# Hybrid decoder trunk on one core: order of the first loads, the step-size projection in fp32 column quarters, and half of the samples' work moved to mid-group in the SSD scan

## The chip, the core and the metric

One NeuronCore of one Trainium2 chip. The metric is the device time of one execution of the whole program in microseconds (us). The kernel before takes 1557.68 us, the median of three runs (1556.93, 1557.68 and 1560.6). One further execution was taken with the hardware profiler.

## The reference

Two layers over 512 prompt tokens and 8 samples of 8 tokens each, all in fp32, model width 1024. Layer 0 has a Conformer convolution beside sliding-window attention; layer 1 has a Mamba-2 mixer. After either comes a gated feed-forward part with a width-3 convolution. The Mamba mixer, where most of the change lies, computes:

```python
z, xbc, dt = jnp.split(h @ w_in, [D_INNER, D_INNER + SSM_CONV_DIM], axis=-1)
xbc = jax.nn.silu(causal_dwconv(concat(conv_hist, xbc), conv_w, conv_b))
xs, bm, cm = jnp.split(xbc, [D_INNER, D_INNER + gn], axis=-1)
dt = jax.nn.softplus(dt + dt_bias)              # 32 heads
y, new_ssm = ssd_scan(xs, dt, -jnp.exp(a_log), bm, cm, ssm_hist)
y = (y + d_skip[:, None] * xs) * jax.nn.silu(z) # then grouped RMSNorm, @ w_out
```

`ssd_scan` cuts the 512 prompt tokens into four chunks of 128. With `acum` the running sum of `dt * a`, it weighs `C B^T` with `exp(acum_l - acum_s)` inside a chunk (the decays), carries a state of 128 x 64 per head from chunk to chunk, and returns the last state. Each sample starts from a state of its own and returns a new one.

## The kernel before

**Layout.** Activations lie with channels on the partitions and the 576 tokens (512 prompt, then 64 sample tokens) along the free axis, in two halves of 288. Every projection is done in three TensorE passes on split operands (`mm3`, lines 166 to 174): a weight tile is rounded to a high part `wh` on ScalarE (L162) and the rest `wl` is made on VectorE (L163); activations are split likewise into `hh` and `hl` (L182, L183). One unit is 128 output channels: 8 blocks x 3 passes x 2 halves = 48 matmuls of 288 columns. Raw weights come through three buffers `wr` (L152), all by the SP queue.

**Order.** The instructions are written out in Python; a compile-time scheduler then gives each engine a fixed order, in which it may take later instructions earlier where it expects their inputs to be ready. DMAs are issued by the SP queue in its own fixed order: an issue that waits for its buffer holds up all behind it.

**Slots.** Working tiles come from a list of slots of one size: 48, and from the first feed-forward part on 11 more (`EXTRA`). `S()` (L65) takes the slot that was freed longest ago; `free()` puts one back at the end of the list. A tile therefore waits for the last reader of whatever lay in its slot before.

**Start.** `setup` (from L108) sends the first weight columns (L152, 256 of them), then the eight x tiles (L126). `mix0` scales and splits each x tile on ScalarE and VectorE (L371, L372).

**Layer 1, `mix1` (from L837).** The norm of h is applied half by half (`norm_half`, L241): `hf = x * gain * rs` (L247), split to `hh`, `hl`. The first three units are then run together: the step sizes dt (256 weight columns, 32 outputs, in 48 matmuls of `mm3` like the others), B and C of group 0; first half 0 of all three, then half 1 (`units`, L257). dt is copied out as `dtr` (L874), transposed to tokens by TensorE (L895, L896), and goes through softplus and running sums to `acd` in DRAM, from which decays are read back broadcast over partitions.

**The scan, `ssd(g)` (L977), four groups of eight heads.** The head of a group: tokens of B (L984); the sample parts (L988 to L1022): copies of B and x for the samples three times over (`r3`), transposed and split into `b3` and `x3`, for both halves of the samples; C B^T masked (`cbm`, L1030); tokens of x times dt (`xdt`, L1037 to L1048, the fifth for the samples); chunk states (L1051 to L1074, the last one stored by L1072); the sample decays `es` (L1076 to L1083). Then four turns t, two heads each: `decays` loads a broadcast row `acb` (L1090), subtracts and exponentiates it on ScalarE (L1094, L1095) and masks it on VectorE (L1096); `outputs` multiplies it with `xdt` into `yp` (L1126); `carried` (L1107 to L1115) prepares the part from the state. `load` (L1141) fetches four sample states, `begin` (L1148, four column quarters of the array) multiplies them with C, `turn` and `finish` (L1165, L1178 to L1182) update and store them: the first four samples after t = 1, the other four after t = 3. Last, `ysp` (L1213) adds the samples' own tokens. `run` (L1253) interleaves this generator, at its yields, with other units (z, or the out-projection of the group before), which fill TensorE.

Of the kernel before, what the change touches and what calls it, by code (L numbers as in the profile page):

```python
# [9 lines left out]
F32R = mybir.dt.float32r  # L10
AF = mybir.ActivationFunctionType
# [3 lines left out]
P = 128  # L15
NP = 512
T = 576
# [23 lines left out]
for _name, _w in (  # L41
    ("ident", 128), ("rsc", 6), ("l1", 128), ("l2", 128), ("h32", 32), ("m32", 32), ("prot", 128), ("blk2", 2), ("blk8", 36), ("amask", 256), ("smask", 2 * 192),
    ("tri", 128), ("tris", 64), ("bmat", 64), ("bsel", 8), ("selx", 256), ("selm", 128),
    ("sel3", 192), ("bsel3", 4),
):
    CV[_name] = _n
    _n += _w
# [3 lines left out]
class Builder:  # L51
    NSLOT = 48
    EXTRA = 11
# [58 lines left out]
    def setup(self):  # L112
        nc, d = self.nc, self.d
        self.par = self.const.tile([P, NPV], F32, name="par")
        self.ident = self.const.tile([P, P], F32, name="ident")
        self.rsc = self.const.tile([P, 6], F32, name="rsc")
        self.l1 = self.const.tile([P, P], F32R, name="l1")
        nc.sync.dma_start(self.par[:, 0:8], d["par"][:, 0:8])
        self.x = []
        for k in range(8):  # L120
            t = self.xp.tile([P, T], F32, tag=f"x{k}", bufs=1, name=f"x{k}")
            self.x.append(t)
        self.pre = []
        self.pre.append(self.weights_load(d["w_in_e"][4][:, 0:256], 256))
        for k in range(8):
            nc.sync.dma_start(self.x[k], d["x"][k])  # L126
            if k == 1:
                nc.sync.dma_start(self.pre[0][:, 256:], d["w_in_e"][4][:, 256:])
            if k == 4:
                self.pre.append(self.weights_load(d["w_in_e"][0], 1024))  # L130
        self.pre.append(self.weights_load(d["w_in_e"][5], 1024))
        nc.sync.dma_start(self.ident, d["cst"][:, 0:128])
        nc.sync.dma_start(self.rsc, d["cst"][:, CV["rsc"]:CV["rsc"] + 6])
        l1 = self.S("l1f")
        nc.sync.dma_start(l1[:, 0:P], d["cst"][:, CV["l1"]:CV["l1"] + P])
# [12 lines left out]
        nc.scalar.activation(warm, self.eps, AF.Sqrt)  # L148
# [75 lines left out]
    def norm_begin(self, gname, early):  # L224
        self.gname, self.early = gname, early
        self.ssq, self.rs = self.S("ssq"), self.S("rs")
        self.h = [self.pair("h") for _ in range(8)]

# [11 lines left out]
    def norm_half(self, half):  # L240
        nc = self.nc  # L241
        sl = HALF[half]
        self.rstd(self.rs, self.ssq, self.o1024, sl)
        if not self.early:
            for k in range(8):
                t = self.S("hf")
                nc.vector.scalar_tensor_tensor(t[:, sl], self.x[k][:, sl], self.pv(self.gname, k), self.rs[:, sl],  # L247
                                               op0=MUL, op1=MUL)
                self.split(t[:, sl], self.h[k], sl)
                self.free(t)  # L250
        if half == 1:
            self.free(self.ssq)
# [4 lines left out]
    def units(self, todo, lead, ready=()):  # L257

        for u0 in (0,) + tuple(range(lead, len(todo))):
            grp = todo[:lead] if u0 == 0 else todo[u0:u0 + 1]  # L260
            ws = ready if ready and u0 == 0 else [self.weights(src, 8 * m) for src, m, _ in grp]
# [575 lines left out]
    def mix1(self):  # L837
# [33 lines left out]
        dtr = self.S("dtr", T, rows=32)  # L871

        def dt_evac(half, p):
            nc.scalar.activation(dtr[:, HALF[half]], p[0:32, :HB], AF.Copy)  # L874
# [19 lines left out]
        for c in range(4):  # L894
            nc.tensor.transpose(pt[:, c * 32:(c + 1) * 32], dtr[:, c * P:(c + 1) * P], self.ident[0:32, 0:32])  # L895
        nc.tensor.transpose(pt[0:64, 128:160], dtr[:, NP:], self.ident[0:32, 0:32])  # L896
# [22 lines left out]
        ea = self.Z("ea", 32, bufs=1)  # L919
# [4 lines left out]
        da = self.Z("da", W, bufs=1)  # L924
        nc.vector.scalar_tensor_tensor(da.rearrange("p (c h) -> p c h", h=32), dt.rearrange("p (c h) -> p c h", h=32), -1.0,
                                       ea.unsqueeze(1).broadcast_to([P, 5, 32]), op0=MUL, op1=MUL)
        dab = self.Z("dab", 256, rows=64, bufs=1)
# [20 lines left out]
        eas = self.Z("eas", 32, rows=64, bufs=1)  # L948
# [7 lines left out]
        dtde, dd3 = self.Z("dtde", 32, rows=64, bufs=1), self.Z("dd3", 64, rows=96, bufs=1)  # L956
# [4 lines left out]
        nc.vector.tensor_copy(dd3, pe[0:96, 0:64])  # L961

# [14 lines left out]
        def ssd(g):  # L977
# [8 lines left out]
            nc.scalar.activation(btok, pt, AF.Copy)  # L986

            r3 = []  # L988
            for a in [bf] + xs:
                r3.append(self.S("r3", 192))  # L990
                nc.scalar.activation(r3[-1].rearrange("p (b r t) -> p b r t", r=3, t=32),
                                     a[:, NP:T].rearrange("p (b t) -> p b t", t=32).unsqueeze(2).broadcast_to([P, 2, 3, 32]),
                                     AF.Copy)
            rep3 = lambda i, bh: r3[i][:, bh * 96:bh * 96 + 96]
            pt = self.ps("pt")
            b3 = []
            for bh in range(2):
                o = pt[0:96, bh * P:(bh + 1) * P]
                nc.tensor.transpose(o, rep3(0, bh), self.ident)
# [3 lines left out]
                b3.append(self.S("b3", NP, F32R, rows=96))  # L1003
# [4 lines left out]
            x3 = []  # L1008
            for bh in range(2):
                pt = self.ps("pt")  # L1010
                for t in range(4):
                    nc.tensor.transpose(pt[0:96, t * P:(t + 1) * P], rep3(1 + t, bh), self.ident)
# [3 lines left out]
                x3.append(self.S("x3", NP, F32R, rows=96))  # L1016
# [3 lines left out]
                yield  # L1020
            self.free(r3)
# [11 lines left out]
            self.free(bf)  # L1033
# [3 lines left out]
            for c in range(5):  # L1037
# [8 lines left out]
                xdt.append(o)  # L1046
                if c % 2:
                    yield  # L1048
# [3 lines left out]
            for c0 in (0, 2):  # L1052
# [9 lines left out]
                for c in (c0, c0 + 1):  # L1062
# [3 lines left out]
                    else:  # L1066
# [9 lines left out]
            es = self.S("es", NP, rows=64)  # L1076
            nc.sync.dma_start(es.rearrange("p (h l) -> p h l", l=64),
                              acd[8 * g:8 * g + 8, NP:T].partition_broadcast(64))
            l64 = lambda ap: ap.rearrange("p (h l) -> p h l", l=64)
            nc.vector.tensor_tensor(l64(es), l64(es), ac[0:64, hs(4)].unsqueeze(2).broadcast_to([64, 8, 64]), op=SUB)  # L1080
            nc.vector.tensor_scalar(es, es, 0.0, None, op0=MIN)
            nc.scalar.activation(es, es, AF.Exp)
            nc.vector.tensor_tensor(l64(es), l64(es), cbm[0:64, NP:].unsqueeze(1).broadcast_to([64, 8, 64]), op=MUL)  # L1083
# [88 lines left out]
            def finish(bh, behind):  # L1172

                for b0 in (0, 2):
# [4 lines left out]
                    self.tc.keep_in_program_order(m)  # L1179
                    for b4 in (b0, b0 + 1):  # L1180
                        nc.vector.tensor_tensor(h0[bh][b4], h0[bh][b4], pst[b4 - b0], op=ADD)
                        nc.sync.dma_start(d["ssm_s"][4 * bh + b4, g], h0[bh][b4])  # L1182
                        self.free(h0[bh][b4])
                    yield

            for t in range(4):
                if t == 0:
                    load(0)
                if t == 0:
                    ea2 = carried(0, False)  # L1190
                pair = []
# [15 lines left out]
                else:  # L1207
                    begin(t // 2)
            ysp = self.ps("ysp", "ysp")
# [9 lines left out]
            self.free(x3, b3)  # L1219
# [110 lines left out]
def constants():  # L1330
# [41 lines left out]
    put("tris", (same & (tt[:, None] <= tt[None, :])).astype(f))  # L1372
    put("bmat", same.astype(f))
# [110 lines left out]
```

## Time and profile before

| what | value |
|---|---|
| median of three runs | 1557.68 us |
| the profiled execution | 1559.9 us |
| its span, first to last instruction | 1558.1 us |
| TensorE (PE) busy | 1525.8 us, 98% |
| VectorE (DVE) busy | 1018.8 us, 65% |
| ScalarE (ACT) busy | 648.9 us, 42% |
| mean granted TensorE clock | 0.995 |
| moved by DMA | 157.78 MB, 101 GB/s |

[...] Busy times of PE are of overlapping matmuls: a busy PE can still run slower than it might, so the start-to-start distance of matmuls is read beside them. A wait is put down to the engine whose signal came last.

### The profile page before, as it was taken

How to read it: one execution, taken by the hardware profiler on the slowest of the kernel's cores; microseconds unless marked ns; L12 is line 12 of the kernel's file. 1: busy time of each engine (PE TensorE's matmuls, PEld its weight loads, DVE VectorE, ACT ScalarE, POOL GpSimd, SP SyncE). 2: the span in 40 equal slices, each digit the busy share in tenths (PEclk: the TensorE clock that was granted, in tenths of full speed). 3: DMA queues.
4: the chain of work that ended last, by engine and by line, in shares of the span. 5: the costliest groups of instructions: out<-in, count | busy, mean ns of one | idle time of the engine just before them, and what ended most of it. 6: DMA issues, size and time to landing. Idle time of an engine off the chain costs nothing.

```text
span 1558.1 us, 28566 instructions
## 1 busy us (share of the span) xinstructions
PE 1525.8 (98%) x11646; PEld 1454.2 (93%) x11646; DVE 1018.8 (65%) x1806; ACT 648.9 (42%) x1233; POOL 154.4 (10%) x365
## 2 busy tenths in 40 slices
PE   7999999999999999999999999999999999999999
PEld 7967799999999999898988988998899999999999
DVE  7968887653555464677896786777976644663552
ACT  6356563221222222576854754656542222221220
POOL 0036001000000000101211102102010000000000
PEclk9999999999999999999999999999999999999999
DMA  8515222222222222136245245235222222223222
GB/s 228 144 42 125 76 82 95 82 84 90 85 77 78 91 82 77 63 94 209 70 141 185 73 126 164 93 115 182 86 82 84 84 90 83 82 72 92 82 85 77
DMA packets 69937, 157.78 MB, mean 101 GB/s; under 512 B 19870, under 2 KB 24606, under 8 KB 69806
## 3 DMA queue, kind: packets, MB, share of 16 engines
q1 hardware_dynamic: 69806, 155.95, 33.1%
q8 instruction: 92, 1.51, 0.4%
q14 instruction: 39, 0.32, 0.1%
HBM read 140.72 MB, written 15.21 MB: 100 GB/s over the span
## 4 chain that ended last, share of the span: by engine, by line
PE 85%; DVE 6%; ACT 5%; DMA 2%; issue 1%; POOL 0%; SPq 0%; ACTq 0%; DVEq 0%
PE mm L172 26%; PE mm L174 26%; PE mm L173 26%; DMA acb<-acd 2%; ACT wh L162 1%; DVE wl L163 1%; ACT acb L1094 1%; PE yp L1126 1%; DVE cconv L863 1%; PE py L1111 1%; PE mm L577 1%; PE pt L1041 1%; ACT sm L644 1%; PE pst L1059 1%; PE pst L1178 0%
## 5 line engine op out<-in xcount | busy, mean ns | idle before, releaser
L172 PE MATMUL mm<-hh,wh 128*128 128x288 f32 x2288 | 681.5, 299 | 8.5 <-ACT hh L371 6.7
L174 PE MATMUL mm<-hh,wl 128*128 128x288 f32 x2288 | 678.2, 297 | 0.6 <-DVE wl L163 0.4
L173 PE MATMUL mm<-hl,wh 128*128 128x288 f32 x2288 | 677.3, 296 | 1.2 <-DVE hl L372 0.7
L162 ACT ACTIVATE wh<-wr 128x1024 fp32r<-128x1024 f32 (+2 forms) x216 | 223.7, 1036 | 547.2 <-PE mm L173 275.7
L172 PEld LDWEIGHTS mm<-hh,wh 128*128 128x128 f32 x2288 | 429.6, 188 | 16.4 <-ACT hh L371 6.7
L173 PEld LDWEIGHTS mm<-hl,wh 128*128 128x128 f32 x2288 | 430.0, 188 | 6.1 <-issue 1.8
L174 PEld LDWEIGHTS mm<-hh,wl 128*128 128x128 f32 x2288 | 430.6, 188 | 3.8 <-issue 1.4
L163 DVE TENSOR_TENSOR wl<-wr,wh 128x1024 fp32r<-128x1024 f32 (+2 forms) x216 | 258.5, 1197 | 76.3 <-ACT wh L162 73.7
L172 PE MATMUL mm<-yh,wh 128*128 128x288 f32 x960 | 286.2, 299 | 1.7 <-DVE x L271 1.4
L174 PE MATMUL mm<-yh,wl 128*128 128x288 f32 x960 | 284.4, 297 | 1.3 <-DVE wl L163 1.3
L173 PE MATMUL mm<-yl,wh 128*128 128x288 f32 x960 | 285.1, 297 | 0.0
L172 PEld LDWEIGHTS mm<-yh,wh 128*128 128x128 f32 x960 | 181.1, 189 | 6.1 <-DVE x L271 2.5
L174 PEld LDWEIGHTS mm<-yh,wl 128*128 128x128 f32 x960 | 181.1, 189 | 2.5 <-DVE wl L163 1.6
L173 PEld LDWEIGHTS mm<-yl,wh 128*128 128x128 f32 x960 | 181.4, 189 | 1.5 <-issue 1.0
L271 DVE TENSOR_TENSOR x<-x,mm 128x288 f32<-128x288 f32 x192 | 84.8, 450 | 145.7 <-PE mm L174 145.6
L316 DVE TENSOR_TENSOR gbuf<-mm,rs 128x224 f32<-128x224 f32 x44 | 17.2, 391 | 108.3 <-PE mm L174 108.3
L327 ACT ACTIVATE gsilu<-gconv,par 128x512 f32<-128x512 f32 x44 | 31.9, 724 | 115.4 <-DVE gconv L324 115.4
L324 DVE SCALAR_TENSOR_TENSOR gconv<-gbuf,par,gconv 128x592 f32<-128x592 f32 x88 | 73.1, 830 | 1.5
L337 DVE TENSOR_TENSOR gsilu<-mm,gsilu 128x288 f32<-128x288 f32 x88 | 40.0, 454 | 50.1 <-PE mm L174 50.1
L863 DVE SCALAR_TENSOR_TENSOR cconv<-cbuf,par,cconv 128x600 f32<-128x600 f32 x72 | 59.6, 838 | 16.1 <-ACT cconv L861 15.5
L319 POOL COPY fpo<-gbuf 128x2 f32<-128x2 f32 x44 | 12.4, 283 | 474.8 <-DVE gbuf L316 474.8
L1094 ACT ACTIVATE acb<-acb,ac 128x128 f32<-128x128 f32 x128 | 41.4, 391 | 32.6 <-DMA acb<-acd 22.7
(320 smaller groups left out, 1595.3 us busy)
## 6 DMA issues: line engine op xcount, KB each, us to landing
wr<-in_w_gate SPq DMA_DIRECT2D x44, 512.0 KB, 3.5
wr<-in_w_up SPq DMA_DIRECT2D x44, 512.0 KB, 3.5
wr<-in_w_in_o SPq DMA_DIRECT2D x40, 512.0 KB, 3.5
wr<-in_w_down SPq DMA_DIRECT2D x32, 448.0 KB, 3.3
wr<-in_w_down SPq DMA_DIRECT2D x16, 512.0 KB, 3.5
h<-in_h SPq DMA_DIRECT2D x32, 256.0 KB, 3.4
acb<-acd SPq DMA_DIRECT2D x32, 256.0 KB, 4.0
out_ssm_s<-h SPq DMA_DIRECT2D x32, 256.0 KB, 2.6
```

The costliest lines, as they stand in the source:

```text
L162: nc.scalar.activation(hi[:, a:b], raw[:, a:b], AF.Copy)
L163: nc.vector.tensor_tensor(lo[:, a:b], raw[:, a:b], hi[:, a:b].bitcast(F32), op=SUB)
L172: nc.tensor.matmul(out, hi[:, ws], xh[:, sl], start=i == 0, stop=False)
L173: nc.tensor.matmul(out, hi[:, ws], xl[:, sl], start=False, stop=False)
L174: nc.tensor.matmul(out, lo[:, ws], xh[:, sl], start=False, stop=i == n - 1)
L271: nc.vector.tensor_tensor(self.x[m][:, sl], self.x[m][:, sl], p[:, :HB], op=ADD)
L316: nc.vector.tensor_tensor(g[:, 290:514], p[:, 0:224], rs[:, HB:NP], op=MUL)
L324: nc.vector.scalar_tensor_tensor(cv[:, :592], g[:, k:592 + k], w(k), cv[:, :592], op0=MUL, op1=ADD)
L327: nc.scalar.activation(sl[:, :NP], cv[:, :NP], AF.Silu, bias=b)
L337: nc.vector.tensor_tensor(sl[:, HALF[half]], p[:, :HB], sl[:, HALF[half]], op=MUL)
L863: nc.vector.scalar_tensor_tensor(cv[:, :600], g[:, k:600 + k], w(k), cv[:, :600], op0=MUL, op1=ADD)
L1094: nc.scalar.activation(acb[:, cs], acb[:, cs], AF.Relu, bias=ac[:, o:o + 1], scale=-1.0)
```

## The change

Five edits. (1) The first x tile is sent ahead of the first weight columns. (2) dt is no longer computed by `mm3`: `hf` is kept in eight slots, the raw fp32 weights are not split, and 16 fp32 matmuls (two rounds of four column quarters per half) leave four partial sums on four partition quarters; the transposes become matmuls with a constant `t32` that adds the quarters. (3) In `ssd`, `parts(bh)` makes `r3`, `b3`, `x3` for one half of the samples: the first at the old place, the second after t = 1; `r3` is one slot in place of five, and `b3`, `x3` are freed in `finish`. (4) The fifth `xdt` is made after t = 2 (`tokens(4)`), the sample decays at the start of t = 2 (`sample_decays`). B (`bf`) is held until `parts(1)`. (5) Some small tiles go from a pool of their own (`Z`) to slots, and `EXTRA` is 12.

```diff
-    EXTRA = 11
+    EXTRA = 12
...
-        self.pre.append(self.weights_load(d["w_in_e"][4][:, 0:256], 256))
         for k in range(8):
             nc.sync.dma_start(self.x[k], d["x"][k])
+            if k == 0:
+                self.pre.append(self.weights_load(d["w_in_e"][4][:, 0:256], 256))
...
+    def quarters(self, p, w, sl):
+        for k in range(2):
+            for q in (3, 2, 1, 0):
+                j = 2 * q + k
+                m = self.nc.tensor.matmul(p[q * 32:q * 32 + 32, :HB], w[:, j * 32:j * 32 + 32], self.hf[j][:, sl],
+                                          start=k == 0, stop=k == 1)
+                if k or q < 3:
+                    self.tc.keep_in_program_order(m)
...
-                t = self.S("hf")
+                if half == 0:
+                    self.hf.append(self.S("hf"))
+                t = self.hf[k]
...
-                self.free(t)
...
-                    self.mm3(p[:m, :HB], w, range(8), self.h, HALF[half], m)
+                    if m == P:
+                        self.mm3(p[:, :HB], w, range(8), self.h, HALF[half])
+                    else:
+                        self.quarters(p, w, HALF[half])
...
-            nc.tensor.transpose(pt[:, c * 32:(c + 1) * 32], dtr[:, c * P:(c + 1) * P], self.ident[0:32, 0:32])
+            nc.tensor.matmul(pt[:, c * 32:(c + 1) * 32], dtr[:, c * P:(c + 1) * P], self.cv("t32", 0, 32), start=True, stop=True)
...
+            def parts(bh):
+                r3 = self.S("r3", 480)
+                for i, a in enumerate([bf] + xs):
+                    nc.scalar.activation(r3[:, i * 96:i * 96 + 96].rearrange("p (r t) -> p r t", t=32),
+                                         a[:, NP + 32 * bh:NP + 32 * bh + 32].unsqueeze(1).broadcast_to([P, 3, 32]), AF.Copy)
...
+            parts(0)
+            yield
             yield
...
-            self.free(bf)
...
-            for c in range(5):
+            def tokens(c):
...
+            for c in range(4):
+                tokens(c)
...
                     self.tc.keep_in_program_order(m)
+                    if b0:
+                        self.free(b3[bh], x3[bh])
...
+                if t == 2:
+                    es = sample_decays()
...
+                if t == 1:
+                    parts(1)
+                    self.free(bf)
+                    yield
+                if t == 2:
+                    tokens(4)
+                    yield
...
-            self.free(x3, b3)
```

## Rows read from the trace of the kernel before

**Rows 1.** The page: span, and busy time of each engine.
```profile
span 1558.1 us, 28566 instructions
PE 1525.8 (98%) x11646; PEld 1454.2 (93%) x11646; DVE 1018.8 (65%) x1806; ACT 648.9 (42%) x1233; POOL 154.4 (10%) x365
```

**Rows 2.** Stretches: length, busy us of PE, PEld, DVE, ACT, POOL; clock, DMA share, GB/s.
```profile
224.00:640.00 416.00, 416.00 (x3142) 415.35 (x3140) 223.41 (x356) 112.72 (x157) 15.66 (x74) 1.00 0.27 83
816.00:837.00 21.00, 19.00 (x146) 18.05 (x145) 13.80 (x23) 8.90 (x21) 0.13 (x1) 0.92 0.68 206
...
955.80:959.20 3.40, 3.40 (x17) 3.40 (x16) 1.85 (x4) 2.21 (x7) 0.00 (x0) 0.50 0.59 222
```

**Rows 3.** Waits of the whole span: us in total, times, longest.
```profile
ACT acb L1094 <- DMA acb<-acd: 22.7, 14, 4.2
...
PE yp L1126 <- DVE acb L1096: 6.6, 5, 2.0
```

**Rows 4.** Timeline, the first 7 us: start, length, engine, line.
```profile
1.18 0.42 SPq L152 DMA_DIRECT2D wr<-in_w_in_e  x1
...
1.65 0.91 SPq L126 DMA_DIRECT2D x<-in_x  x2
...
3.35 0.42 ACT L162 ACTIVATE wh<-wr 128x256 fp32r<-128x256 f32 x1 [1.12 <-DMA wr<-in_w_in_e]
...
5.89 0.77 ACT L371 ACTIVATE hh<-x,par 128x576 fp32r<-128x576 f32 x1 [2.12 <-DMA x<-in_x]
...
6.72 0.85 PE L172 MATMUL mm<-hh,wh 128*128 128x288 f32 x2 [6.72 <-ACT hh L371]
```

**Rows 5.** Timeline of PE and DVE around half 1 of dt, B, C.
```profile
651.71 0.30 PE L174 MATMUL mm<-hh,wl 128*128 128x288 f32 x1
653.13 0.58 PE L172 MATMUL mm<-hh,wh 128*32 128x288 f32 x3 [1.13 <-ACT hh L182]
...
657.91 0.89 DVE L183 TENSOR_TENSOR hl<-hf,hh 128x288 fp32r<-128x288 f32 x2
...
663.21 0.31 PE L895 MATMUL pt<-ident,dtr 32*128 32x32 f32 x2
```

**Rows 6.** Timeline of PE: four column quarters of 512 columns, and what follows.
```profile
840.60 1.07 PE L1148 MATMUL pyo<-h,cfm 128*32 128x512 f32 x8
841.59 0.40 PE L172 MATMUL mm<-hh,wh 128*128 128x288 f32 x1
841.83 0.30 PE L173 MATMUL mm<-hl,wh 128*128 128x288 f32 x1
```

**Rows 7.** Line 953, two fp32 matmuls of 32 columns: shortest, median, longest ns; first and last start.
```profile
L953 PE MATMUL pe<-eas,cst x4: 189/272/273, 678.2 to 678.5; 64*128 64x32 f32 x4
```

**Rows 8.** SP queue, group 1, turns t = 0 to 2.
```profile
817.08 0.82 SPq L1141 DMA_DIRECT2D h<-in_h  x2
817.99 0.38 SPq L1090 DMA_DIRECT2D acb<-acd  x1
...
828.29 2.53 SPq L1090 DMA_DIRECT2D acb<-acd  x2
831.09 0.94 SPq L1182 DMA_DIRECT2D out_ssm_s<-h  x2
```

**Rows 9.** ACT and PE in the same turns.
```profile
823.20 1.28 ACT L1094 ACTIVATE acb<-acb,ac 128x128 f32<-128x128 f32 x4 [3.77 <-DMA acb<-acd]
...
825.94 1.88 PE L1126 MATMUL yp<-acb,xdt 128*64 128x128 f32 x16 [2.00 <-DVE acb L1096]
...
837.79 0.44 PE L1126 MATMUL yp<-acb,xdt 128*64 128x128 f32 x4 [0.58 <-DVE acb L1096]
```

**Rows 10.** The page's DMA issues: KB each, us to landing.
```profile
acb<-acd SPq DMA_DIRECT2D x32, 256.0 KB, 4.0
out_ssm_s<-h SPq DMA_DIRECT2D x32, 256.0 KB, 2.6
```

**Rows 11.** Groups by form: busy us, mean ns | idle before.
```profile
L1083 DVE TENSOR_TENSOR es<-es,cbm 64x512 f32<-64x512 f32 x4 | 2.7, 680 | 1.3 <-ACT es L1082 1.3
```

More of the change, by code (lines that the diff above doesn't have):

```diff
@@ L43 @@
     ("tri", 128), ("tris", 64), ("bmat", 64), ("bsel", 8), ("selx", 256), ("selm", 128),
-    ("sel3", 192), ("bsel3", 4),
+    ("sel3", 192), ("bsel3", 4), ("t32", 32),
 ):
@@ L227, in norm_begin @@
         self.h = [self.pair("h") for _ in range(8)]
+        self.hf = []
     def norm_tile(self, m, sl):
@@ L260, in units @@
             grp = todo[:lead] if u0 == 0 else todo[u0:u0 + 1]
-            ws = ready if ready and u0 == 0 else [self.weights(src, 8 * m) for src, m, _ in grp]
+            ws = ready if ready and u0 == 0 else [self.weights(src, 8 * m) if m == P else self.weights_load(src, 8 * m)
+                                                  for src, m, _ in grp]
             for half in (0, 1):
@@ L869, in conv_evac @@
             return go
-        dtr = self.S("dtr", T, rows=32)
+        dtr = self.S("dtr")
         def dt_evac(half, p):
-            nc.scalar.activation(dtr[:, HALF[half]], p[0:32, :HB], AF.Copy)
+            nc.scalar.activation(dtr[:, HALF[half]], p[:, :HB], AF.Copy)
+            if half:
+                self.free(self.hf)
         bfm, cfm, xss, zss = {}, {}, {}, {}
@@ L894, in mix1 @@
         for c in range(4):
-            nc.tensor.transpose(pt[:, c * 32:(c + 1) * 32], dtr[:, c * P:(c + 1) * P], self.ident[0:32, 0:32])
-        nc.tensor.transpose(pt[0:64, 128:160], dtr[:, NP:], self.ident[0:32, 0:32])
+            nc.tensor.matmul(pt[:, c * 32:(c + 1) * 32], dtr[:, c * P:(c + 1) * P], self.cv("t32", 0, 32), start=True, stop=True)
+        nc.tensor.matmul(pt[0:64, 128:160], dtr[:, NP:], self.cv("t32", 0, 32), start=True, stop=True)
         self.free(dtr)
@@ L918, in mix1 @@
         nc.vector.scalar_tensor_tensor(dt, q, 2.0, v, op0=MUL, op1=ADD)
-        ea = self.Z("ea", 32, bufs=1)
+        ea = self.S("ea", 32)
         zero = self.Z("zero", 1, bufs=1)
@@ L923, in mix1 @@
         self.free(v, e, z, z2, q)
-        da = self.Z("da", W, bufs=1)
+        da = self.S("da", W)
         nc.vector.scalar_tensor_tensor(da.rearrange("p (c h) -> p c h", h=32), dt.rearrange("p (c h) -> p c h", h=32), -1.0,
                                        ea.unsqueeze(1).broadcast_to([P, 5, 32]), op0=MUL, op1=MUL)
-        dab = self.Z("dab", 256, rows=64, bufs=1)
+        dab = self.S("dab", 256, rows=64)
         nc.vector.tensor_tensor(dab.rearrange("p (b h) -> p b h", h=32),
@@ L947, in mix1 @@
         nc.scalar.activation(cds, pb[:, 160:416], AF.Exp)
-        eas = self.Z("eas", 32, rows=64, bufs=1)
+        eas = self.S("eas", 32, rows=64)
         nc.scalar.activation(eas, ac[0:64, 128:160], AF.Exp)
@@ L954, in mix1 @@
         nc.vector.tensor_copy(eax, pe[:, 0:64])
-        dtde, dd3 = self.Z("dtde", 32, rows=64, bufs=1), self.Z("dd3", 64, rows=96, bufs=1)
+        dtde, dd3 = self.S("dtde", 32, rows=64), self.Z("dd3", 64, rows=96, bufs=1)
         nc.vector.tensor_tensor(dtde, dt[0:64, 128:160], de[0:64, 128:160], op=MUL)
@@ L961, in mix1 @@
         nc.vector.tensor_copy(dd3, pe[0:96, 0:64])
+        self.free(ea, da, dab, eas, dtde)
         acr = self.S("acr", T, rows=32)
@@ L986, in ssd @@
             nc.scalar.activation(btok, pt, AF.Copy)
[L988 to L999, printed above, removed]
+            b3, x3 = {}, {}
+            def parts(bh):
[3 more added lines that the diff above has]
+                                         a[:, NP + 32 * bh:NP + 32 * bh + 32].unsqueeze(1).broadcast_to([P, 3, 32]), AF.Copy)
+                pt = self.ps("pt")
+                o = pt[0:96, 0:P]
+                nc.tensor.transpose(o, r3[:, 0:96], self.ident)
                 bp = self.S("bp", P, F32R, rows=96)
@@ L1002, in ssd @@
                 nc.vector.tensor_tensor(bp[64:96, :], o[64:96, :], bp[64:96, :].bitcast(F32), op=SUB)
-                b3.append(self.S("b3", NP, F32R, rows=96))
+                b3[bh] = self.S("b3", NP, F32R, rows=96)
                 nc.vector.tensor_tensor(b3[bh].rearrange("p (b n) -> p b n", n=P),
@@ L1007, in ssd @@
                 self.free(bp)
-            x3 = []
-            for bh in range(2):
                 pt = self.ps("pt")
-                for t in range(4):
-                    nc.tensor.transpose(pt[0:96, t * P:(t + 1) * P], rep3(1 + t, bh), self.ident)
+                for t in (3, 0, 1, 2):
+                    m = nc.tensor.transpose(pt[0:96, t * P:(t + 1) * P], r3[:, (1 + t) * 96:(2 + t) * 96], self.ident)
+                    if t < 3:
+                        self.tc.keep_in_program_order(m)
+                self.free(r3)
                 xf = self.S("xf", NP, rows=96)
@@ L1015, in ssd @@
                                         dd3[:, bh * 32 + 8 * g:bh * 32 + 8 * g + 8].unsqueeze(2).broadcast_to([96, 8, 64]), op=MUL)
-                x3.append(self.S("x3", NP, F32R, rows=96))
+                x3[bh] = self.S("x3", NP, F32R, rows=96)
                 nc.scalar.activation(x3[bh], xf, AF.Copy)
@@ L1019, in ssd @@
                 self.free(xf)
-                yield
-            self.free(r3)
+            parts(0)
+            yield
             yield
@@ L1074, in ssd, with sample_decays @@
             yield
-            es = self.S("es", NP, rows=64)
-            nc.sync.dma_start(es.rearrange("p (h l) -> p h l", l=64),
-                              acd[8 * g:8 * g + 8, NP:T].partition_broadcast(64))
             l64 = lambda ap: ap.rearrange("p (h l) -> p h l", l=64)
[L1080 to L1083, printed above, removed]
+            def sample_decays():
+                es = self.S("es", NP, rows=64)
+                nc.sync.dma_start(es.rearrange("p (h l) -> p h l", l=64),
+                                  acd[8 * g:8 * g + 8, NP:T].partition_broadcast(64))
+                nc.vector.tensor_tensor(l64(es), l64(es), ac[0:64, hs(4)].unsqueeze(2).broadcast_to([64, 8, 64]), op=SUB)
+                nc.vector.tensor_scalar(es, es, 0.0, None, op0=MIN)
+                nc.scalar.activation(es, es, AF.Exp)
+                nc.vector.tensor_tensor(l64(es), l64(es), cbm[0:64, NP:].unsqueeze(1).broadcast_to([64, 8, 64]), op=MUL)
+                return es
             yo = []
@@ L1188, in ssd @@
                     load(0)
-                if t == 0:
                     ea2 = carried(0, False)
+                if t == 2:
+                    es = sample_decays()
                 pair = []
@@ L1372, in constants @@
     put("tris", (same & (tt[:, None] <= tt[None, :])).astype(f))
+    put("t32", np.tile(np.eye(32, dtype=f), (4, 1)))
     put("bmat", same.astype(f))
```

## The prediction

> **What bounds it now.** I read the page first: PE is busy for 1525.8 of 1558.1 us, DVE for 1018.8 [rows 1]. So the question is what PE does in its few gaps, and how much work it is spared. The view by stretches says where the gaps are not: in the feed-forward part from 224 to 640 us PE is busy for all of 416.00 us, and its 3142 matmuls make 0.132 us each, start to start [rows 2]. That is the price of a 288-column pass, and nothing can be won there. In layer 1 it is different. From 816 to 837 us (group 1 of the scan) PE is busy for 19.00 of 21.00 us, at a mean clock of 0.92 [rows 2]; a clock short by 0.08 over 21 us is 1.7 us lost. In group 2 the clock stands at 0.50 from 955.80 to 959.20 us [rows 2], another 1.7 us. The waits name the cause: PE waits 6.6 us, in five waits, at L1126 for the masked decays `acb`, and ACT waits 22.7 us for their DMA [rows 3]. The timeline shows one such chain. The SP queue issues two sample-state loads at 817.08, behind them an `acb` at 817.99 [rows 8]; ACT gets it at 823.20, after 3.77 us of idling, and PE starts `yp` at 825.94, after 2.00 us [rows 9]. The loads ahead of it write into slots that the turn before has to free, and SP goes in order. So slots that are freed late make loads late, and late loads stop PE. That is 6.6 + 2 x 1.7 = 10.0 us in the scan, the largest sum that the change can reach.
>
> **The start.** Today the first 256 weight columns are issued at 1.18 and rounded at 3.35, while ACT has nothing else; the first x tile, issued at 1.65, is split at 5.89, and PE starts at 6.72 [rows 4]. Swapped, x is issued 0.47 us earlier, but the 0.42 us of rounding moves from an idle stretch into ACT's work on x. The bytes of both are the same, so both are there by 5.89 at the latest; then 0.42 us of rounding gives 6.31 for the weights against 6.66 (5.89 + 0.77) for x today. I take 0.4 us gained, between 0 (all queues shared, nothing earlier) and 1.0 (x earlier by its place and the bytes ahead of it).
>
> **dt.** 48 matmuls at 0.132 us go: 6.4 us of PE. In come four rounds of four column quarters in fp32. The nearest row is such a round of 512 columns: 840.60 to 841.59, 0.99 us [rows 6]; for 288 columns I scale to 0.56, between that and 0.99 unscaled. The matmul after it runs 0.24 us to the next start (841.59 to 841.83 [rows 6]) in place of 0.13, so leaving the quarters costs 0.11. Four rounds and two exits: 2.5 us, at most 4.4. [...] The row shows 0.11, and the sum uses that. Saved: 3.9 us, half of it in either half.
>
> What of it reaches the end is read around half 1. After half 0 PE starts its last matmul at 651.71 and the next only at 653.13, waiting for `hh` [rows 5]: the norm of half 1 is late, and DVE and ACT make it. Half 0's 1.95 us only lengthen this wait, to some 3.2 us: gain 0. From 653.13, B and C need 48 x 0.132 = 6.4 us and the quarters 1.2: 660.7. VectorE's last `hl` ends at 658.80 [rows 5], so production no longer lags far behind. Today dt's transposes follow at 663.21 [rows 5]: gain 2.4. The transposes become fp32 matmuls. Line 953 has two in four records within 0.3 us of starts, so 0.2 us each, five make 1.0 [rows 7]; two of today's take 0.31 with their tail [rows 5], five some 0.4 to 0.8. I charge 0.6, of 0.2 to 1.0. **Term: 1.8 us gained**, between 0 (below) and 3.7 (all of it on the path). The unsplit weights spare ACT and DVE a short piece each that nobody waits for. They hold one of the three raw buffers until the last quarter; the load that took it now takes B's, read out before half 0 starts, and its unit runs behind half 1, so I charge nothing; were it late, PE would wait at 660.7. The eight `hf` slots fall in a time of many free slots.
>
> **The scan.** Counted along the slot list of group 1, before the change `acb` of t = 1 comes into a slot of the last chunk state, behind its store, and the second four sample states into the slots of t = 0's `acb`. After it, four fewer slots are held in the head (one `r3` for five, no second `b3` and `x3`, no fifth `xdt`, no `es`, B one longer, one slot more), and t = 1's `acb` gets slots that the head has long left. Its load can go some turns earlier, and the five waits at L1126 with both stretches at half clock can go: 10.0 us, the lower end of this term being 0.
>
> What is late next? Counted on, the second `acb` of t = 2 falls on the slot of the first stored sample state. That store is issued at 831.09 and lands 2.6 us later [rows 8, 10], at 833.7; today the two `acb` of t = 2 are issued from 828.29 to 830.8 [rows 8]. So it comes some 3 us later, and PE, which at t = 2 waits 0.58 us today [rows 9], could wait up to 3.8. Against that t = 1 ends 2.0 us sooner, and other units fill. I take 1.2 us in each of four groups, 4.8 in all, between 0 and 3.8 each. The moved pieces are some seven VectorE operations of 0.68 us a group [rows 11], 4.8 us, out of the head into t = 1 to 3; from 816 to 837 us DVE is idle for 7.2 of 21 us [rows 2], which hides them. Without that cover each delays the mask L1096, and PE behind it, by up to 0.7 us. ACT's copies for `r3` double in number at half the size, and ACT is idle for 12.1 of those 21 us. SP gets no DMA more; the `es` load moves behind the first `acb` loads, which helps these. **Term: 10.0 - 4.8 = 5.2 us gained**, from 10 gained to 5 lost.
>
> **Sum.** 0.4 + 1.8 + 5.2 = 7.4 us off the profiled execution's own time of 1559.9, to 1552.5. That execution lies 2.2 us above the median of 1557.7; from the median I forecast **1550.3 us**. A difference of 0.3% (4.7 us) is about what a measurement of this kernel can tell from no change.
>
> **Rivals.**
> *The loads stay late (0.24).* The 16 DMA engines are busy for 0.68 of the stretch from 816 to 837 us [rows 2], and an `acb` needs 4.0 us to land [rows 10]. If the traffic, not the slot, makes it late, the scan gains nothing: 2.2 us in all, 1555.5. For it speaks that ACT got the row of 817.99 only 5.2 us later [rows 8, 9]; against it, that it was also issued late.
> *The second wait takes over (0.12), slower.* The `acb` behind the state store, at t = 2 in all four groups, stops PE for the full 3.8 us, and its clock falls each time as after the 2.00 us wait, 1.7 more: 4 x 5.5 = 22 us, less 10.0 and 2.2: 1567.5. It decides once the units beside it run out before the load lands. Against it: today's wait there is 0.58 us.
> *dt's gain is taken back by the clock (0.16).* The wait before half 1 grows to some 3.2 us, longer than the 2.00 us after which PE fell to half clock in group 1. One fall costs 1.7 us: dt is worth 0.1, and the time is 1552.0. [...]
> *No new wait (0.13).* The scan gives all 10.0: 1545.5.
>
> **Chances and range.** The forecast has 0.35. Faster by over 0.3%: 0.35 + 0.16 + 0.13, less 0.02 for the end of the forecast's own spread, 0.62; within 0.3%: 0.24 + 0.02 = 0.26; slower: 0.12. The range runs from 1544.0 (the case of no new wait with 1.5 us more) to 1557.0 (the late loads with dt at nothing); it leaves out the slower case and some 0.05 at the ends.
>
> **What would show it.** Right: PE's first start near 6.3; 16 fp32 matmuls of 32 output columns in place of 48, ending near 661 rather than 663; `acb` of t = 1 issued before the first `yp` of its group, no wait over 1 us at L1126 in groups 1 and 2 at t = 1, and no clock of 0.50 near 826 and 956. Wrong: waits at L1126 of as many us as today, now at t = 2, behind a state store; a half-clock stretch near 652; or `acb` loads issued early that land as late as now.

## The result: slower, with the profile after

| what | before | after |
|---|---|---|
| median of 17 runs each | 1556.62 us | 1563.2 us |
| the profiled execution | 1559.9 us | 1560.62 us |
| mean granted TensorE clock in it | 0.995 | 0.993 |

The ratio is 1.0045, with a 95% interval from 1.0035 to 1.0056: the changed kernel is slower by some 6.6 us, outside the range. The two profiled executions lie only 0.7 us apart, since that of before is one of its longer ones and that of after one of its shorter ones. So I read the profiles by stage, and the medians for the sum.

The page of after, beside [rows 1]: span, instructions, and busy time of each engine.

```profile
span 1558.8 us, 28590 instructions
...
PE 1524.3 (98%) x11635; PEld 1452.2 (93%) x11635; DVE 1020.1 (65%) x1805; ACT 658.8 (42%) x1259; POOL 159.7 (10%) x365
```

Nothing shows here: TensorE is busy for 1.5 us less and the span is 0.7 us longer. The timeline of the first 7 us, beside [rows 4]:

```profile
1.19 0.42 SPq L125 DMA_DIRECT2D x<-in_x  x1
...
1.65 0.43 SPq L153 DMA_DIRECT2D wr<-in_w_in_e  x1
...
4.15 0.78 ACT L388 ACTIVATE hh<-x,par 128x576 fp32r<-128x576 f32 x1 [1.92 <-DMA x<-in_x]
...
4.83 0.40 ACT L163 ACTIVATE wh<-wr 128x256 fp32r<-128x256 f32 x1
...
5.28 0.85 PE L173 MATMUL mm<-hh,wh 128*128 128x288 f32 x2 [5.28 <-ACT wh L163]
```

The first matmul now waits for the weights, as forecast, and starts at 5.28 us, 1.44 earlier. TensorE around the two halves of dt, beside [rows 5, 6]:

```profile
644.40 0.29 PE L174 MATMUL mm<-hl,wh 128*128 128x288 f32 x1
644.62 1.18 PE L182 MATMUL mm<-hf,wr 128*32 128x288 f32 x16
645.73 0.40 PE L173 MATMUL mm<-hh,wh 128*128 128x288 f32 x1
645.97 0.29 PE L174 MATMUL mm<-hl,wh 128*128 128x288 f32 x1
...
651.25 0.40 PE L218 MATMUL pr<-dg,l 128*128 128x288 f32 x1 [1.10 <-DVE dg L214]
653.18 0.53 PE L173 MATMUL mm<-hh,wh 128*128 128x288 f32 x2 [1.53 <-ACT hh L193]
...
659.23 1.18 PE L182 MATMUL mm<-hf,wr 128*32 128x288 f32 x16
```

Two rounds of quarters take 1.11 us (644.62 to 645.73; each fp32 matmul leaves two records, so eight appear as 16), and TensorE then waits 1.10 and 1.53 us for the norm of half 1. The clock follows: in the view by stretches, the same 3.4 us are at 1.00 before (first row) and at 0.51 after (second row), while the stretches of [rows 2] in groups 1 and 2 are at full clock in this execution:

```profile
654.10:657.50 3.40, 3.40 (x27) 2.90 (x26) 3.40 (x10) 1.38 (x4) 1.29 (x5) 1.00 0.00 0
...
654.10:657.50 3.40, 3.40 (x15) 3.40 (x16) 3.40 (x10) 1.33 (x4) 0.00 (x0) 0.51 0.00 0
816.00:837.00 21.00, 19.77 (x167) 18.18 (x165) 17.28 (x29) 10.99 (x28) 0.74 (x1) 1.00 0.68 209
955.80:959.20 3.40, 3.40 (x28) 3.40 (x27) 1.09 (x2) 1.30 (x3) 3.40 (x3) 1.00 0.47 126
```

The waits of TensorE in the whole span, after, beside [rows 3]; the last row is the wait for `wl` before:

```profile
PE mm L175 <- DVE wl L164: 4.2, 3, 1.9
PE yp L1153 <- DVE acb L1123: 3.1, 3, 1.3
...
PE mm L174 <- DVE wl L163: 1.8, 2, 1.3
```

The wait for `acb` fell from 6.6 to 3.1 us, and the first `yp` of group 3 starts at 1044.93 us, at 1060.70 before. But the wait for low weight parts `wl` rose from 1.8 to 4.2 us. What this does to TensorE, the stretches of the tail show, first after, then before:

```profile
1083.00:1090.00 7.00, 4.38 (x31) 3.93 (x31) 5.68 (x14) 3.22 (x8) 0.30 (x3) 0.59 0.24 75
1090.00:1097.00 7.00, 6.02 (x42) 5.01 (x38) 5.71 (x15) 3.92 (x9) 0.00 (x0) 0.92 0.00 0
1097.00:1104.00 7.00, 4.43 (x15) 3.56 (x16) 6.68 (x11) 1.83 (x5) 0.00 (x0) 0.56 0.23 69
```

```profile
1083.00:1090.00 7.00, 6.67 (x55) 6.08 (x50) 6.47 (x17) 1.51 (x2) 0.00 (x0) 1.00 0.39 150
1090.00:1097.00 7.00, 5.87 (x55) 5.20 (x54) 7.00 (x21) 5.65 (x12) 0.62 (x5) 1.00 0.11 28
1097.00:1104.00 7.00, 5.65 (x29) 5.37 (x30) 6.38 (x16) 2.50 (x7) 0.00 (x0) 0.76 0.25 75
```

In these 21 us TensorE ran 139 matmuls before (99 of them passes of 288 columns) and 88 after (61 of them), at clocks down to 0.56. The waits that open those holes, on the timeline of TensorE after (the first row is the last `yp` of the scan):

```profile
1073.47 1.09 PE L1153 MATMUL yp<-acb,xdt 128*64 128x128 f32 x16
...
1083.71 0.33 PE L202 MATMUL pt<-gssq,o 128*32 128x72 f32 x8 [1.31 <-DVE gssq L229]
1085.95 0.61 PE L175 MATMUL mm<-yh,wl 128*128 128x288 f32 x1 [1.91 <-DVE wl L164]
...
1101.22 0.61 PE L175 MATMUL mm<-yh,wl 128*128 128x288 f32 x1 [1.69 <-DVE wl L164]
```

The out-projection of group 2 comes in four weight blocks of 48 matmuls each; they are TensorE's filler while the gate of group 3 is worked out on VectorE and ScalarE. In both kernels the program writes the third and fourth block behind `gate(3)`; it is the scheduler that may take their weights ahead of it. On ScalarE and VectorE after, the third block's `wh` and `wl`, the gate's products (L1280), the fourth block's `wl`, and the first result of the second feed-forward part (L329):

```profile
1053.16 1.06 ACT L163 ACTIVATE wh<-wr 128x1024 fp32r<-128x1024 f32 x1 [2.62 <-PE mm L174]
...
1083.57 1.19 DVE L1280 TENSOR_TENSOR xs<-xs,zs 128x288 f32<-128x288 f32 x3
1084.68 1.22 DVE L164 TENSOR_TENSOR wl<-wr,wh 128x1024 fp32r<-128x1024 f32 x1
...
1099.95 1.22 DVE L164 TENSOR_TENSOR wl<-wr,wh 128x1024 fp32r<-128x1024 f32 x1
...
1139.50 0.39 DVE L329 TENSOR_TENSOR gbuf<-mm,rs 128x288 f32<-128x288 f32 x1
```

And before, the `wl` of the third and fourth block, with the gate between them:

```profile
1061.77 1.22 DVE L163 TENSOR_TENSOR wl<-wr,wh 128x1024 fp32r<-128x1024 f32 x1 [1.69 <-ACT wh L162]
...
1083.36 0.45 DVE L1244 TENSOR_TENSOR xs<-xs,zs 128x288 f32<-128x288 f32 x1
...
1097.74 1.16 DVE L163 TENSOR_TENSOR wl<-wr,wh 128x1024 fp32r<-128x1024 f32 x1
...
1137.67 0.45 DVE L312 TENSOR_TENSOR gbuf<-mm,rs 128x288 f32<-128x288 f32 x1
```

Before, the third `wl` follows its `wh` at once. After, it comes 30 us behind its `wh` (1054.22 to 1084.68), behind products of the gate: VectorE works in the order that the scheduler fixed, and after the change it no longer took this split ahead of the gate. From the last `yp` (1082.69 before, 1073.47 after) to the first result of the feed-forward part it is 55.0 us before and 66.0 after. The 9.2 us that the scan was ahead are spent there, and 1.8 more.

How much of the loss is waiting and how much is clock can be estimated from the granted clocks of all executions. Their mean is 0.9926 in the 17 of the changed kernel and 0.9971 in the 78 of before that ran beside the experiments below. If TensorE loses what the clock is short of 1, that is 11.6 us against 4.5, a difference of 7 us: about the whole loss. By this estimate the waits in the tail only use up what the change had gained, and the falls to half clock (from 1084 and from 1098 us in the profile after, some 6.8 us each, against one of 3.4 from 1099 before) make it slower.

### The profile page after: what moved, and what is told of

The parts are those of the page before. It is cut to its first block, busy times and chain, and to the rows that moved or that the text cites. A ratio compares the mean times of both kernels' runs of the same rounds, so it can differ in the third digit from the quotient of the medians.

```text
span 1558.8 us, 28590 instructions
## 1 busy us (share of the span) xinstructions
PE 1524.3 (98%) x11635; PEld 1452.2 (93%) x11635; DVE 1020.1 (65%) x1805; ACT 658.8 (42%) x1259; POOL 159.7 (10%) x365
## 4 chain that ended last, share of the span: by engine, by line
PE 42%; DVE 4%; DMA 3%; ACT 2%; issue 1%; SPq 0%; ACTq 0%; DVEq 0%
PE mm L175 13%; PE mm L173 13%; PE mm L174 13%; DMA acb<-acd 1%; DVE wl L164 1%; DMA out_ssm_s<-h 1%; ACT wh L163 1%; PE yp L1153 1%; DMA ea<-acd 0%; PE pst L1082 0%; DVE xs L1284 0%; ACT acb L1121 0%; DMA h<-in_h 0%; PE pst L1205 0%; DVE acb L1123 0%
## 5 line engine op out<-in xcount | busy, mean ns | idle before, releaser
L1181 POOL TENSOR_TENSOR h<-h,cds 128x512 f32<-128x512 f32 x32 | 43.8, 1399 | 149.3 <-PE pyo L1175 50.0
```

The lines of the kernel that those rows point to most:

```text
L1181: nc.gpsimd.tensor_tensor(hp(h0[bh][b4]), hp(h0[bh][b4]), cds[:, b * 32 + 8 * g:b * 32 + 8 * g + 8].unsqueeze(2).broadcast_to([P, 8, 64]), ...
```

## The experiments

First the parts, each alone. The working theory was that the scan edits lose in the last gate what they gain.

**First x tile first (edit 1 alone).**

```diff
+            if k == 0:
+                self.pre.append(self.weights_load(d["w_in_e"][4][:, 0:256], 256))
```

> Before with edit 1 alone (x first). Theory A (the scan edits pay in groups 1 and 2 and give it back in the last gate; the quarters are worth nothing; the start is worth what the first matmul shows): the first matmul near 5.3 us in place of 6.7, and 1.0 to 1.5 us off the time of the kernel before. Theory B (the loss is not in the scan but in the start and the quarters): no gain, or a loss of some us. Theory C (no part costs anything by itself; the whole changes the work so that the clock granted is lower all over): within 1 us of before.

Ratio 0.9989 (0.9978 to 1.0): 1.7 us faster, at the edge of what can be told. The first matmul starts at 5.34 us. In the other five profiles without this edit it starts at 5.62, 5.66, 5.70, 5.76 and 6.09 us, in all eight with it between 5.24 and 5.35: the 6.72 of [rows 4] was one late landing, and the edit is worth some 0.4 us at this place.

**dt in fp32 quarters (edit 2 alone).**

```diff
-                    self.mm3(p[:m, :HB], w, range(8), self.h, HALF[half], m)
+                        self.quarters(p, w, HALF[half])
```

> Before with edit 2 alone (dt in fp32 quarters). Theory A: PE waits about 3 us for the norm of half 1, in two pieces, a stretch at 0.50 comes near 655 us, dt is copied out at the same time as before, and the time is within 1 us of before. Theory B: 3 to 6 us slower than before, with more than the one stretch of 3.4 us at 0.50. Theory C: within 1 us, but the mean clock lower.

Ratio 0.9987 (0.9976 to 0.9998): 2.0 us faster (0.3 to 3.7), more than theory A allowed, though the stretch at 0.50 came at 652.9 us. dt is copied out no earlier against the start of the norm (20.91 us behind it, 20.85 before), but TensorE has some 3.7 us less to do (48 passes at 0.132 less two visits of 1.31, below), and the x units behind it start earlier. In its profile the first `yp` of group 0 starts at 713.52 us, 2.6 us earlier than in before (716.10), where the norm ahead of it was 0.7 us later. That this is the way the gain takes is read from one profile of each, not shown by a run.

**The scan alone (edits 3 to 5).**

```diff
+    EXTRA = 12
...
+                if t == 1:
+                    parts(1)
...
+                if t == 2:
+                    tokens(4)
```

> Before with edits 3 to 5 alone (second half of the samples and their decays in mid-group, 12 extra slots). Theory A: the first yp of group 3 some 13 to 16 us earlier than before, the stretches at 0.50 near 826 and 956 gone, two long ones between 1080 and 1105 in their place; in the end 4 to 7 us slower than before. Theory B: 3 to 8 us faster than before, the tail of group 3 as before. Theory C: the groups as in A, the end within 2 us.

Ratio 1.0047 (1.003 to 1.0064): the whole loss is here, as theory A said. The first `yp` of group 3 is 12.7 us early (a little less than expected), the last 6.7 us (1076.03 for 1082.69), and the two waits for `wl` in the tail, 1.91 and 1.90 us, are those of the changed kernel. One thing theory A missed: a stretch at 0.50 stands at 952.3 us, behind the wait at t = 2 of group 2.

**The changed kernel with mm3 for dt.**

```diff
-                        self.quarters(p, w, HALF[half])
+                        self.mm3(p[:m, :HB], w, range(8), self.h, HALF[half], m)
```

> The changed kernel with edit 2 undone (dt by the three passes again). Theory A: no stretch at 0.50 near 655; the losses in the tail of group 3 stay: within 2 us of the changed kernel, that is 3 to 6 us slower than before. Theory B: 4 to 8 us faster than the changed kernel, so faster than before. Theory C: between the two, with the clock.

Ratio 1.0045 (1.0029 to 1.0061), and no stretch at 0.50 near 655: the quarters are not the cause. Theory B falls.

The next runs ask what the loss in the tail hangs on: the place of two splits in VectorE's order (D), or the mere lack of filler (E).

**The changed kernel, weights of the third and fourth block ahead of the gate.**

```diff
+            if g == 3:
+                for c in (2, 3):
+                    ws[c] = self.weights(srcs[c], 1024)
             ys = gate(g, xs)
```

> The changed kernel with one thing moved: the weights of the third and fourth column block of group 2's out-projection are split ahead of gate(3) in program order, not behind it. Theory D (in the tail of group 3 TensorE has enough matmuls left but their low weight parts wl stand behind the gate's work in VectorE's fixed order): no wait of 1.9 us for wl and no 6.8 us at 0.50 between 1080 and 1105; 7 to 10 us faster than the changed kernel, 1550 to 1556 in the profile, so 2 to 5 us faster than before. Theory E (the scan ends earlier, so too few matmuls are left beside the gate, whatever their weights do): within 2 us of the changed kernel, the gaps only move behind the last out tile.

1552.97 us, ratio 0.997 (0.996 to 0.9981): 4.7 us faster than before, and 10.2 us faster than the changed kernel by the medians. VectorE and the same three stretches:

```profile
1074.89 1.21 DVE L164 TENSOR_TENSOR wl<-wr,wh 128x1024 fp32r<-128x1024 f32 x1
...
1082.91 1.22 DVE L164 TENSOR_TENSOR wl<-wr,wh 128x1024 fp32r<-128x1024 f32 x1
1084.04 1.56 DVE L1280 TENSOR_TENSOR xs<-xs,zs 128x288 f32<-128x288 f32 x4
```

```profile
1083.00:1090.00 7.00, 5.27 (x46) 4.87 (x44) 7.00 (x17) 4.60 (x11) 0.30 (x3) 1.00 0.25 75
1090.00:1097.00 7.00, 7.00 (x49) 6.53 (x48) 5.12 (x15) 3.76 (x9) 0.00 (x0) 0.76 0.01 2
1097.00:1104.00 7.00, 6.14 (x43) 5.52 (x42) 7.00 (x18) 3.18 (x6) 0.00 (x0) 1.00 0.16 58
```

Both splits now stand ahead of the gate's products, TensorE gets 138 matmuls into the 21 us in place of 88 (115 passes of 288 columns in place of 61), and from the last `yp` to the first `gbuf` it is 57.6 us (1074.65 to 1132.26). The edit moves the loads and the roundings of the two blocks in the program as well, but in the trace their `wh` keep their places (1054.35 and 1071.54 us, against 1053.16 and 1070.35), and the last `yp` is only 1.2 us later. The matmuls were there all along; E falls.

**Before, with the third block's split behind the gate's products.**

```diff
+                            with self.tc.issue_after(self.gated):
+                                ws[2] = self.weights(srcs[2], 1024)
```

> Before with the low weight part of the third column block of group 2's out-projection queued on VectorE behind the four products of the gate's first half (as the changed kernel has it). Theory D: TensorE waits 2 us or more for it near 1090, its clock falls to 0.50 there, and the time is 3 to 8 us over before, without any of the change's edits. Theory E: within 2 us of before, since the matmuls are there anyway.

Ratio 1.0016 (1.0004 to 1.0028): 2.5 us slower (0.6 to 4.4), between the bounds of E and D, so the time does not tell them apart; the trace speaks for D. In it only the third block's `wl` is late: its `wh` stands at 1057.85, and its `wl` comes at 1090.31. The two waits on TensorE's timeline are those of the changed kernel, and the clock is at 0.50 from 1088.7 to 1095.5 us:

```profile
1089.35 0.47 PE L191 MATMUL pt<-gssq,o 128*32 128x72 f32 x8 [2.05 <-DVE gssq L218]
1091.59 0.61 PE L174 MATMUL mm<-yh,wl 128*128 128x288 f32 x1 [1.77 <-DVE wl L163]
```

So this order makes a part of the loss in a kernel with none of the change's edits. From the last `yp` to the first `gbuf` it is 59.8 us (1079.08 to 1138.91), against 55.0 and 66.0. Only one long wait for `wl` came here, as in before (1.35 us, for the fourth block), where the changed kernel has two; before with both blocks late was not tried.

**Before, with the two splits ahead of the gate.**

```diff
+                for c in (2, 3):
+                    ws[c] = self.weights(srcs[c], 1024)
```

> Before with the same move as the repaired changed kernel (third and fourth block's weights split ahead of gate(3)). Theory D: before has one such wait (for the fourth block, near 1098, with 3.4 us at 0.50), so 1 to 3 us faster than before, not more. Theory E: within 1 us of before.

Ratio 0.9997 (0.9985 to 1.0009): nothing that can be told, as theory E said and not theory D, though a gain of up to 2.3 us lies within the interval. The stretch at 0.50 that before has from 1099.1 us is gone and the wait for the fourth block is down from 1.35 to 0.6 us, but before had the third block in place already. The move repairs the change; no gain by itself is shown.

**The changed kernel, group 3 in the old order.**

```diff
-                if t == 1:
+                if t == 1 and g < 3:
                     parts(1)
...
-                if t == 2:
+                if t == 2 and g < 3:
                     tokens(4)
```

> The changed kernel with group 3 in the old order (both halves of the samples, all tokens and the sample decays in the head; mid-group only in groups 0 to 2). Theory D: what counts is where VectorE's order puts the third block's wl; it stands there behind two or four gate products, before ysp, so the tail costs less than in the changed kernel: 3 to 8 us faster than it. Theory E: the scan of group 3 ends later by the moved work, the tail is covered again: 5 to 8 us faster.

1553.94 us, ratio 0.9982 (0.997 to 0.9995). Leaving group 3 alone cannot be told from the repair by the intervals, and by the medians it is 9.3 us faster than the changed kernel, more than either theory allowed. The time does not tell D from E, but the trace does: the scan hardly ends later than in the changed kernel (last `yp` at 1074.09, against 1073.47), as E would need it to, while the third `wl` starts at 1076.07 in place of 1084.68, behind three gate products in place of eight, and TensorE no longer waits for `wl` there.

Then the terms of the sum, with the tail repaired.

**Edits 1 and 2 together; edits 3 to 5 with the repair.** Their edits are those shown above.

> Before with edits 1 and 2 together, no scan edit. If the parts add up: ratio 0.998 to 0.996 to before (0.9989 and 0.9987 were measured alone), that is 3 to 6 us faster, and the repaired changed kernel owes little to the scan edits. If they share one gain (both only shift the phase in which later loads and the clock fall): no better than either alone, 1 to 2 us faster.

> Before with edits 3 to 5 and the two weight splits ahead of gate(3); no start, no quarters. If the scan edits are worth what the trace shows until the last group ends (some 3 us beyond what start and quarters bring): 2 to 4 us faster than before. If their gain was only borrowed from the tail (other units run later, TensorE's work is the same): within 1.5 us of before.

Ratios 0.9987 (0.9973 to 1.0001) and 0.998 (0.9966 to 0.9994). Start and quarters together are 2.0 us faster, at the edge of what can be told, so it stays open whether they add up: 0.9976 would lie within the interval. The scan edits, 7.3 us slower alone, are 3.1 us faster (0.9 to 5.3) with the two splits moved.

**The repaired kernel, another slot for the second `acb` of t = 2.**

```diff
+                    if t == 2 and hh == 1 and g in (1, 2):
+                        self.idle.insert(0, self.idle.pop(2))
```

> The repaired changed kernel, and in groups 1 and 2 the second acb of t = 2 takes a slot that b3 has left in place of the first stored sample state's. If the store in that slot makes the load late (my forecast's mechanism): no wait over 1 us for acb at t = 2, no 0.50 near 950, and 2 to 4 us faster than the repaired kernel in the profile. If the load is late for another reason (SP's order, the traffic): the wait stays, within 1 us.

1549.8 us, ratio 0.9952 (0.994 to 0.9964). That is 3.2 us under the repaired kernel by the medians, as the first theory said, but the two intervals still meet (0.996 to 0.9964), so the gain is likely and not certain. The half clock near 950 us that the repaired kernel has is gone too; the changed kernel, with the old slot, had none there either, so this proves little. The waits at t = 2 did not go: 2.38 us ahead of the `yp` at 832.52 and 1.77 ahead of that at 951.06, against 0.80 and 2.62 without the swap. SP's queue in group 2:

```profile
935.79 0.33 SPq L1117 DMA_DIRECT2D acb<-acd  x1
...
938.48 3.21 SPq L1211 DMA_DIRECT2D out_ssm_s<-h  x4
941.79 1.08 SPq L1117 DMA_DIRECT2D acb<-acd  x1
```

The second `acb` is now issued as soon as the four state stores are out, but it still stands behind them in SP's order, and ScalarE gets it only at 947.47, 5.7 us later, against 4.0 in [rows 10]. Without the swap it was issued 3.0 us after the last store and landed 3.6 later. So of 2.9 us that the slot cost, 2.1 come back as a slower landing, and `yp` of t = 2 follows that of t = 1 only 0.8 us sooner (17.70 against 18.53). In group 1, where the load went out at 823.10 between the second and the third store, `yp` came 1.0 us sooner (15.64 against 16.61 behind that of t = 1). So in the trace the slot is a small part. Whether the rest is the stores in front or the traffic was not tested: a load moved ahead of all four stores was not tried.

**The same, with the first x unit of group 0 beside dt, B and C.**

```diff
-        self.units([(d["w_dt"], 32, dt_evac)] + bc_units(0), 3)
+        bc0 = bc_units(0)
+        xu0 = x_units(0)
+        self.units([(d["w_dt"], 32, dt_evac)] + bc0 + xu0[:1], 4)
...
-        self.units(x_units(0), 1)
+        self.units(xu0[1:], 1)
```

> As the run before, and the first x unit of group 0 runs with dt, B and C (four units together in place of three), so that TensorE has 48 more matmuls before the norm of half 1 is needed. If the wait there takes back the quarters' gain: no wait of over 0.5 us and no 0.50 near 653, 2 to 4 us faster than the run before. If the later step sizes then hold up the head of group 0, or half 1 is late anyway: within 1 us, or slower.

1549.26 us, ratio 0.995 (0.9934 to 0.9966), not told apart from the run before by its time; its six runs go from 1544.39 to 1552.81. In the profile the step does what was asked, in the view by stretches:

```profile
640.00:662.00 22.00, 21.93 (x175) 18.80 (x174) 17.18 (x39) 12.78 (x31) 1.22 (x3) 1.00 0.23 64
```

TensorE is busy for 21.93 of the 22 us around half 1, and between the first 15 us and the end no stretch at 0.50 is left; this execution took 1544.39 us. With the run before it is the fastest version here, 7.5 and 7.8 us under before by the ratios.

## Why the prediction was wrong, step by step

**The sum** failed, at the step that carried the scan's term to the end. I wrote that SP's late loads and the waits at L1126 cost 10.0 us in the scan, that 4.8 would come back at t = 2, and that "other units fill". I never costed what stands behind group 3, where those other units run out and the gate's work decides in what order VectorE hands TensorE its weights. Measured, the scan term is 7.3 us lost instead of 5.2 gained, although up to the last `yp` the scan edits alone are 6.7 us ahead. With the two splits back in front of the gate it is 3.1 gained, and the whole change 4.7 (3.0 to 6.2) in place of 7.4. So the loss hangs on where two VectorE instructions of 1.22 us each stand, which the change does not touch. Undoing this order in the changed kernel takes the whole loss away; making it in before, for one of the two, brings 2.5 us (0.6 to 4.4) of it. That the scheduler chose that order because the scan ended earlier in its own reckoning is argued, not shown.

**The waits at L1126.** Right for t = 1: the last `acb` of t = 1 in group 1 is issued at 805.20, before the group's first `yp` at 807.83, and no wait is left there. But I had read the five waits of before wrongly. Only three stand at t = 1 (2.00, 1.28 and 0.91 us in groups 1 to 3); 0.58 us in group 1 and 1.84 in group 2 stand at t = 2, and the half clock from 955.80 follows the 1.84:

```profile
943.37 1.09 PE L1126 MATMUL yp<-acb,xdt 128*64 128x128 f32 x16 [1.28 <-DVE acb L1096]
...
954.47 1.09 PE L1126 MATMUL yp<-acb,xdt 128*64 128x128 f32 x16 [1.84 <-DVE acb L1096]
```

These are t = 1 and t = 2 of group 2 before; t = 1 and t = 2 of group 1 are in [rows 9]. So of the 10.0 us some 5.9 (4.2 of waits and one stretch of 1.7) hung on the loads that the edits free, and the other 4.1 on t = 2. There the waits did not come new, they rose from 2.4 to 3.2 us (1.13, 1.34 and 0.68 in groups 1 to 3), where I charged 1.2 in each of four groups. The cause that I gave, the slot of the first stored state, is in the trace only a part of it: with another slot the waits stayed. The signs of the clock were weak ones. Half clock near 826 comes in three of the six profiles with the old scan and in none of the eight with the new one, but near 950 to 959 it comes in four of six and in five of eight. The repaired kernel, with the same scan as the changed one, is among these, behind its wait of 2.62 us; that the changed kernel's profile has none there is no sign for the edits.

**The start.** 0.4 us forecast; 0.4 by the first matmul over many runs, though the single profile of before showed 1.44. That the first matmul then hangs on the rounded weights is as forecast. That the size fits is in part luck: x is split some 0.6 us or more sooner (4.10 to 4.21 us against 4.80 to 5.89 in the profiles without the edit), which the sum left to its upper bound, and the rounding waits for that split, which it left out.

**dt.** The price was right: 1.11 us for two rounds and 0.24 to the next start, where the sum had 1.12 and 0.11 more than the usual 0.13. TensorE is spaced 0.22 us before the quarters and 0.24 behind them, against 0.13 in the stream: entering and leaving cost about 0.2 us a visit; what TensorE does in that time is not shown. Wrong was where the gain shows: I expected dt's transposes 2.4 us early (2.5 by the figures that I gave), and they came at 662.97, 0.24 us early; VectorE reads their result at 663.76, where before it was 663.77, so on this path the gain is nothing. The rival of the clock took place as written: a wait (2.6 us, 3.2 forecast) and, after its two pieces, a stretch at 0.51 (654.10 to 657.50 us in the changed kernel). Still the edit alone is worth 2.0 us (0.3 to 3.7), about the 1.8 of the term and by luck, since the gain comes by another way: the work saved lets the x units behind it start early, as far as the profiles show.

**The rivals.** The slower side got 0.12 and the wrong mechanism: a second wait at t = 2 that takes over, 22 us. A wait did take over, but for `wl` in the tail. "The loads stay late" is out, since the loads came early. Of the signs that I named for the changed kernel, none lay behind group 3. The range had a slip too: the late loads with dt at nothing give 1557.3 us, not 1557.0; it decides nothing here.

## What to carry to other kernels

When a change makes one stage shorter, follow the time to the next place where the filler of the bounding engine runs out, and look there at the order in which the helper engines serve it. An order fixed at compile time can change far from the edit: compare the new order of the small producing instructions (here two weight splits) with the old one before believing a sum of removed waits. A gain that fits in the trace up to one group and is gone at the end is a matter of that seam, and a move of a few lines can decide its sign.

## What the runs showed of the hardware that was not expected

A wait and a fall of the clock do not go together as simply as I took it from [rows 2, 9]. With the other slot TensorE waited 2.38 us before the `yp` at 832.52 and no stretch at 0.50 followed, and with dt in quarters alone it waited 7.2 us in five pieces at `yp` without one; in before the 2.00 us ahead of the `yp` at 825.94 had one behind them (0.53 from 825.90 to 829.30 us), in the changed kernel the 2.6 us in two pieces near 652 (0.51 from 654.10 to 657.50 us). In such a stretch a pass of 288 columns takes 0.24 us from start to start (1086.36 to 1086.60 in the changed kernel) where it takes 0.13 otherwise.

The first transfers of the program land at different times from execution to execution: without the swap the first split of x starts between 4.80 and 5.89 us in six profiles, with it between 4.10 and 4.21 in the eight.
